# RMSNorm and matmul on one core: the first eight output tiles in one store in place of two

## Chip, core and metric

The kernel runs on one core of a Trainium2 chip. The metric is device time in microseconds (us). Before the change the median of three runs is 209.02 us (208.88 to 209.29).

## What is computed

Each of 16 x 1024 = 16,384 tokens has 512 features. A token is divided by the root of its mean square, scaled by gamma, and multiplied by a 512 x 768 weight matrix, all inputs and outputs in f32:

```python
def reference(x, gamma, weight, eps):
    rms = np.sqrt(np.mean(x ** 2, axis=-1, keepdims=True) + eps)
    x_norm = x / rms * gamma
    return np.matmul(x_norm, weight).astype(np.float32)
```

33.6 MB of tokens come in and 50.3 MB of results go out, so besides the arithmetic a good 85 MB pass through the core's 16 DMA engines.

## The kernel before

**Tiles.** The tokens are cut into NT = 128 tiles of 128 tokens, one token per partition. Tiles 2j and 2j+1 are pair j, and the main loop runs over pairs. A tile is loaded as f32 (`xt`), cast to bf16 by GpSimd (`xb`, line 189), transposed by TensorE as f32 words that each hold two bf16 (line 231), copied from PSUM to `xT` by VectorE (`evac`, line 240), multiplied with the weights in eight matmuls (line 300) into one of three PSUM accumulators taken in turn, and scaled by 1/rms on the way out of PSUM into `ot` (`scale`; even tiles on ScalarE, line 279, odd tiles on VectorE, line 281). ScalarE also makes the sums of squares (line 197) and the square roots (line 202). Gamma is multiplied into the weights at the start.

**Quads.** From tile 28 on, the last four of every 16 tiles (28 to 31, 44 to 47, ..., 124 to 127) take another way to their transposed form: GpSimd casts all four into `xq` (`cast_quad`, line 260), and VectorE transposes them in 16 blocks (`move_quad`, line 271), three blocks at the head of each pair, before the pair's other VectorE work. The quad of tiles 124 to 127 is cast at pair 55 and first moved at pair 56, which is tiles 112 and 113.

**Loads.** `x_first` and `x_size` say which tiles travel together: tiles 0 to 3, tiles 4 to 7, and from then on eight tiles a transfer. The loads of the first 32 tiles and the weights are issued on SP (SyncE) at the start; later ones on ScalarE's queue, in ScalarE's program order, when the pair loop reaches them (`load_until`). `xt` holds two blocks of 16 tiles.

**Stores.** `o_first` and `o_size` do the same for the output. When the last tile of a group is scaled, `store` issues the group's transfer on SP, from one of four `ot` buffers of eight tiles. SP issues in order and a wait of one store holds only later stores. `finish_tile` makes the last tile of a group also wait for the tile before it.

**Which token is where.** `rows` gives the view of `x` or of `out` for a transfer: within a block of `t` tiles, partition p holds `t` tokens that lie side by side in memory. The same function serves loads and stores, so a tile has the same tokens in both. A partition's share of a load is 2 KB a tile, of a store 3 KB a tile.

**The order of instructions** is written out by hand: each operation is recorded with the cells that it reads and writes (class `Order`), and semaphore waits are derived from them; no scheduler moves anything.

Of the kernel before, what the change touches and what calls it, by code (L numbers as in the profile page):

```python
# [100 lines left out]
def kernel(  # L101
# [22 lines left out]
    XG, OG = 16, 8  # L124
# [3 lines left out]
    def stretches(group, parts):  # L128
        first, size, i = {}, {}, 0
        for g in range(NT // group):  # L130
            for n in parts.get(g, [group]):
                for t in range(i, i + n):
                    first[t], size[t] = i, n
                i += n
        return first, size

    last = NT // OG - 1
    x_first, x_size = stretches(OG, {0: [4, 4]})
    o_first, o_size = stretches(OG, {0: [4, 4], last - 1: [4, 4], last: [4, 2, 2]})

    def rows(ap, i, n):
        base, t = (i - i % OG, OG) if OG <= i < XG else (x_first[i], x_size[i]) if i < OG else (i - i % XG, XG) if i < 2 * XG else (i - i % (2 * XG), 2 * XG)
        return ap[base * P:(base + t) * P, :].rearrange("(p t) d -> p t d", t=t)[:, i - base:i - base + n, :]

    def sb(name, shape, dtype):
# [29 lines left out]
    def load(i):  # L175
        dst, to = x_of(i, x_size[i])
        queue = SP if i < FIRST else ACT
        order.transfer(queue, lambda: queue.dma_start(out=dst, in_=rows(x, i, x_size[i])), writes=to)
# [109 lines left out]
    def store(i):  # L288
        first, n = o_first[i], o_size[i]
        s = first // OG % OTS  # L290
        if i == first + n - 1:
            src = ot[s][:, first % OG:first % OG + n, :]
            order.transfer(SP, lambda: SP.dma_start(out=rows(out, first, n), in_=src), reads=cells("ot", s, first % OG, n))
# [188 lines left out]
```

## Time and profile before

| | |
|---|---|
| median of the runs | 209.02 us |
| the profiled execution, its own time | 208.72 us |
| its span, first to last instruction | 206.8 us |
| TensorE busy | 193.7 us (94%) |
| VectorE busy | 149.3 us (72%) |
| ScalarE busy | 144.8 us (70%) |
| GpSimd busy | 60.2 us (29%) |
| DMA | 85.62 MB, 414 GB/s over the span |
| granted TensorE clock | 0.987 |
| stores | 13 of 3072 KB, 5 of 1536 KB, 2 of 768 KB, all on SP |
| loads on ScalarE's queue | 12 of 2048 KB, median 19.4 us from issue to landing |

Engines are PE (TensorE matmul), PEld (its weight load), DVE (VectorE), ACT (ScalarE), POOL (GpSimd) and SP (SyncE). Line numbers such as L281 are those of the kernel before. The profile numbers the DMA queues: q1 is SP's, q10 is ScalarE's. A transfer is spread over the 16 DMA engines, eight partitions to each; a partition's share moves as one piece, which the trace records with start, duration and size. Times are counted from the start of the span. The median time from issue to landing contains the time that a transfer stands in its queue.

### The profile page before, as it was taken

The page shows a single profiled execution, that of the slowest core. Times are in us where ns is not written, and L with a number is a line of the kernel's source. Part 1 is how long each engine was busy: PE and PEld are TensorE (multiplying, and loading weights), DVE is VectorE, ACT ScalarE, POOL GpSimd, SP SyncE. Part 2 cuts the span into 40 slices and gives each one's busy share as a digit, 9 for nine tenths or more (in the row PEclk, how much of TensorE's full clock was granted, in tenths as well). Part 3 has the DMA queues.
Part 4 walks back from the last instruction along what each step waited for, and adds up shares of the span by engine and source line. Part 5 has one row for each costly group of instructions (what it writes and reads, how often), then busy time and mean ns, then how long its engine had stood idle before and what let it go on. Part 6 is the DMA issues. An engine that isn't in the chain of part 4 may idle for free.

```text
span 206.8 us, 2750 instructions
## 1 busy us (share of the span) xinstructions
PE 193.7 (94%) x1212; PEld 72.8 (35%) x717; DVE 149.3 (72%) x255; ACT 144.8 (70%) x343; POOL 60.2 (29%) x34
## 2 busy tenths in 40 slices
PE   7799999999999999999999999999999999999920
PEld 0244433433433333433343333343343334343300
DVE  0446557998579966999579975999569974999410
ACT  2698998877777687777787687677877688663310
POOL 1437733154206250153305160060704206000000
PEclk9999999999999999999999999999999999999995
DMA  5999999999999999999999999999999999999992
GB/s 206 426 436 437 393 390 431 428 445 429 436 425 415 441 434 431 439 428 425 418 431 442 417 444 415 441 428 425 444 428 420 441 428 431 433 428 416 423 412 103
DMA packets 5632, 85.62 MB, mean 414 GB/s; under 512 B 626, under 2 KB 628, under 8 KB 1140
## 3 DMA queue, kind: packets, MB, share of 16 engines
q1 hardware_dynamic: 3888, 60.29, 68.8%
q10 hardware_dynamic: 1732, 25.17, 28.5%
q8 instruction: 7, 0.11, 0.2%
q14 instruction: 5, 0.04, 0.0%
HBM read 35.13 MB, written 50.33 MB: 413 GB/s over the span
## 4 chain that ended last, share of the span: by engine, by line
PE 91%; DMA 2%; DVE 1%; issue 1%; ACT 1%; SPq 0%
PE ps L300 80%; PE ps L231 10%; DMA xt<-in_x_dram 2%; DVE ot L281 0%; ACT jk L197 0%; DVE xT L240 0%; DVE w_bf L281 0%; ACT ssq L202 0%; DVE rstd L204 0%; SPq L477 0%; SPq L436 0%
## 5 line engine op out<-in xcount | busy, mean ns | idle before, releaser
L300 PE MATMUL ps<-w_bf,xT 128*128 128x256 bf16 (+1 forms) x783 | 145.1, 326 | 1.1 <-DVE w_bf L281 0.2
L279 ACT ACTIVATE ot<-ps,rstd 128x768 f32<-128x768 f32 x64 | 57.7, 901 | 46.2 <-PE ps L300 46.1
L197 ACT ACTIVATE jk<-xt 128x512 bf16<-128x512 f32 x128 | 78.9, 620 | 3.1 <-DMA xt<-in_x_dram 3.1
L189 POOL CAST xb<-xt 128x2048 bf16<-128x2048 f32 (+3 forms) x21 | 46.4, 2221 | 108.3 <-DMA xt<-in_x_dram 56.5
L281 DVE TENSOR_SCALAR ot<-ps,rstd 128x768 f32<-128x768 f32 x64 | 64.8, 1013 | 9.7 <-PE ps L300 9.2
L296 PEld LDWEIGHTS <-xT 128*128 128x128 bf16 x400 | 39.3, 98 | 59.4 <-issue 57.9
L231 PE MATMUL ps<-ident_f,xb 128*128 128x128 f32 x200 | 54.4, 276 | 1.1 <-POOL xb L189 1.1
L240 DVE COPY xT<-ps 128x1024 bf16<-128x1024 bf16 (+1 forms) x53 | 34.5, 653 | 25.5 <-PE ps L231 24.9
L271 DVE STREAM_TRANSPOSE xTq<-xq 32x256 f32<-32x256 f32 x112 | 48.7, 435 | 1.9
L231 PEld LDWEIGHTS ps<-ident_f,xb 128*128 128x128 f32 x200 | 28.2, 143 | 46.5 <-issue 43.6
L300 PE MATMUL ps<-w_bf,xTq 128*128 128x256 bf16 (+1 forms) x217 | 41.8, 324 | 0.4
L197 ACT ACTIVATION_READ_ACCUMULATOR jk<-xt 128x1 f32 x128 | 24.5, 192 | 0.0
L296 PEld LDWEIGHTS <-xTq 128*128 128x128 bf16 x112 | 11.0, 98 | 14.5 <-issue 14.5
L260 POOL CAST xq<-xt 128x2048 bf16<-128x2048 f32 x7 | 13.3, 1896 | 4.6 <-DVE xTq L271 4.6
L204 DVE RECIPROCAL rstd<-ssq 128x8 f32<-128x8 f32 (+3 forms) x20 | 3.9, 193 | 7.5 <-ACT ssq L202 7.4
L202 ACT ACTIVATE ssq<-ssq,eps_sb 128x8 f32<-128x8 f32 (+3 forms) x20 | 6.0, 302 | 0.6
L300 PE MATMUL ps<-ot 128*128 128x512 bf16 x10 | 4.8, 628 | 1.4 <-DVE eps_sb L354 1.4
L279 ACT ACTIVATE w_bf<-ot,g_sb 128x768 bf16<-128x768 f32 x2 | 1.9, 937 | 1.1 <-DMA ot<-in_weight_dram 1.1
L377 DVE COPY g_sb<-ps 128x4 f32<-128x4 f32 x1 | 0.2, 161 | 3.1 <-PE ps L371 3.1
L341 ACT ACT_TABLE_LOAD x1 | 1.3, 1283 | 1.5 <-SPq L436 1.5
L281 DVE TENSOR_SCALAR w_bf<-ot,g_sb 128x512 bf16<-128x512 f32 (+2 forms) x3 | 1.4, 483 | 0.6 <-DMA ot<-in_weight_dram 0.6
L371 PEld LDWEIGHTS ps<-ident_f,ot 2*128 2x128 f32 x2 | 0.3, 200 | 2.6 <-issue 2.6
(10 smaller groups left out, 2.0 us busy)
## 6 DMA issues: line engine op xcount, KB each, us to landing
out_dram<-ot SPq DMA_DIRECT2D x13, 3072.0 KB, 23.9
xt<-in_x_dram ACTq DMA_DIRECT2D x12, 2048.0 KB, 19.4
out_dram<-ot SPq DMA_DIRECT2D x5, 1536.0 KB, 10.8
xt<-in_x_dram SPq DMA_DIRECT2D x3, 2048.0 KB, 18.4
xt<-in_x_dram SPq DMA_DIRECT2D x2, 1024.0 KB, 7.3
ot<-in_weight_dram SPq DMA_DIRECT2D x2, 768.0 KB, 7.0
out_dram<-ot SPq DMA_DIRECT2D x2, 768.0 KB, 7.3
ot<-in_gamma_dram ACTq DMA_DIRECT2D x1, 2.0 KB
```

The costliest lines, as they stand in the source:

```text
L189: run(POOL, lambda: POOL.tensor_copy(out=xb[s][:, i % 8:i % 8 + n, :], in_=src), of, cells("xb", s, i % 8, n))
L197: run(ACT, lambda: ACT.activation(out=jk[n], in_=src[:, 0, :], func=AF.Square, accum_out=ssq[:, i:i + 1]), of, [("jk", n), ("ssq", i)])
L202: run(ACT, lambda: ACT.activation(out=ssq[:, s], in_=ssq[:, s], func=AF.Sqrt, scale=1.0 / D, bias=eps_sb), [("ssq", t) for t in range(i, i ...
L204: run(DVE, lambda: DVE.reciprocal(out=rstd[:, s], in_=ssq[:, s]), [("rms", i)], [("rstd", t) for t in range(i, i + n)])
L231: run(PE, lambda: PE.transpose(out=tp[b][:, t, h, :], in_=words[:, lo:lo + P], identity=ident_f), cells("xb", s, j % 4 * 2 + t) + ["ident" ...
L240: run(DVE, lambda: DVE.tensor_copy(out=dst[:, t:t + n, :], in_=src[:, t:t + n, :]), [("tp", b)], cells("xT", j % XTS, t, n))
L260: run(POOL, lambda: POOL.tensor_copy(out=xq, in_=src), of, ["xq"])
L271: run(DVE, lambda: DVE.transpose(out=dst, in_=src), ["xq"], [("xTq", n)])
L279: run(ACT, lambda: ACT.mul(out=dst, in_=src, mul=r), reads, writes)
L281: run(DVE, lambda: DVE.tensor_single_scalar(out=dst, in_=src, scalar=r, op=mybir.AluOpType.mult), reads, writes)
L296: run(PE, lambda: PE.ldweights(lhsT), of)
L300: run(PE, lambda: PE.add_instruction(mybir.InstMatmult(name=nc.get_next_instruction_name(), engine=mybir.EngineType.PE, ins=[PE.lower_ap(r ...
```

## The change

Tiles 0 to 7 are stored by one transfer of 3072 KB, issued when tile 7 is ready, where tiles 0 to 3 and 4 to 7 were stored by two of 1536 KB. For this the eight tokens of a partition must lie side by side in memory, so the view in `rows` changes for tiles 0 to 7: a block is now eight tiles. It holds for the loads too. Tiles 0 to 7 are still loaded by two transfers of four tiles (`x_first`, `x_size` are as they were), but each now takes one half of every partition's eight tokens: pieces of 8 KB that lie 16 KB apart, where they adjoined. The instructions of TensorE, VectorE, ScalarE and GpSimd are the same ones in the same order; SP has one store less. Tile 3 is no longer the last of a group, so its scaling no longer waits for tile 2.

```diff
     last = NT // OG - 1
     x_first, x_size = stretches(OG, {0: [4, 4]})
-    o_first, o_size = stretches(OG, {0: [4, 4], last - 1: [4, 4], last: [4, 2, 2]})
+    o_first, o_size = stretches(OG, {last - 1: [4, 4], last: [4, 2, 2]})
 
     def rows(ap, i, n):
-        base, t = (i - i % OG, OG) if OG <= i < XG else (x_first[i], x_size[i]) if i < OG else (i - i % XG, XG) if i < 2 * XG else (i - i % (2 * XG), 2 * XG)
+        base, t = (i - i % OG, OG) if i < XG else (i - i % XG, XG) if i < 2 * XG else (i - i % (2 * XG), 2 * XG)
         return ap[base * P:(base + t) * P, :].rearrange("(p t) d -> p t d", t=t)[:, i - base:i - base + n, :]
```

## The prediction, made before the changed kernel was run

> **What bounds the kernel now.** I read the page's busy slices and its chain of waits first, then busy time by stretch, then the stores at the end. In the slices (40 of them, tenths busy) TensorE's row and the DMA row are both full; the chain of waits names TensorE.
>
> ```profile
> PE   7799999999999999999999999999999999999920
> DMA  5999999999999999999999999999999999999992
> PE 91%; DMA 2%; DVE 1%; issue 1%; ACT 1%; SPq 0%
> ```
>
> The chain follows instructions and can't see that a transfer stands in line behind others. The stretches can (columns: stretch and its length, busy time and instructions of PE, PEld, DVE, ACT and POOL, granted clock, DMA share, GB/s):
>
> ```profile
> 22.70:24.20 1.50, 1.45 (x12) 0.59 (x7) 1.50 (x3) 0.99 (x4) 1.50 (x1) 1.00 1.00 426
> 24.20:27.30 3.10, 3.10 (x23) 1.28 (x14) 1.65 (x3) 3.10 (x9) 1.41 (x1) 1.00 0.98 308
> 110.00:170.00 60.00, 59.63 (x383) 22.52 (x224) 50.12 (x85) 45.67 (x111) 18.28 (x7) 1.00 1.01 431
> 170.00:198.00 28.00, 27.50 (x175) 9.95 (x100) 20.49 (x35) 15.62 (x32) 3.73 (x2) 1.00 1.00 425
> 198.00:205.50 7.50, 0.00 (x0) 0.00 (x0) 0.77 (x1) 0.00 (x0) 0.00 (x0) 0.72 0.64 265
> ```
>
> The DMA share is 0.98 to 1.01 up to 198 us, at 425 to 431 GB/s apart from one dip, and TensorE has nothing left after 198. What fills 198 to 205.5 is a line of stores. The last two, by issue time and by time to landing:
>
> ```profile
> 196.20 0.33 SPq L293 DMA_DIRECT2D out_dram<-ot  x1
> out_dram<-ot SPq DMA_DIRECT2D x1, 768.0 KB, 7.8
> 199.06 0.33 SPq L293 DMA_DIRECT2D out_dram<-ot  x1
> out_dram<-ot SPq DMA_DIRECT2D x1, 768.0 KB, 6.8
> ```
>
> They land at 204.0 and 205.9, 1.9 us apart, though issued 2.9 apart. The records of single transfers say why: a DMA engine moves one partition's 6 KB of these stores in 0.234 us, eight make 1.88 us. Read engine by engine, all 16 move data without a pause from 3 us to about 202; most end between 202 and 203.6 and one, which also fetches instructions, ends at 205.41. That engine sets the end. Its eight pieces of the last store start at 203.53; issued at 199.06, and with the 1.0 us from issue to first data that the first load shows (0.95 to 1.95), they could have started at 200.06. So **TensorE has about 3.4 us of slack** to the end: 3.5 by the last store, 3.4 by the store issued at 193.59 (starts 197.96). The time is set by the bytes, and by anything that leaves that DMA engine idle.
>
> **The change part by part.** *Removed:* one store issue on SP (0.33 us, SP otherwise waits: nothing), one completion write per DMA engine (0.009 us each), and VectorE's wait on ScalarE at tile 3 (ScalarE had long finished tile 2: nothing). *Merged:* per DMA engine 16 pieces of 12 KB at 0.4613 us (7.38) become 8 pieces of 24 KB at 0.9154 (7.32), by the mean of such pieces in this trace: 0.06 us less. With the completion write, **-0.07 us**.
>
> *Loads of tiles 0 to 7:* still two transfers in pieces of 8 KB, but now 16 KB apart instead of adjoining. No row shows that. The nearest: pieces of 16 KB that adjoin (tiles 8 to 15) and that lie 32 KB apart (tiles 16 to 31) both take 0.613 us. I take nothing; the bound is one more slow start like that of the first loads (2 to 4 us; 0.5 us over the normal 0.309 a piece, summed over 16 engines), so 0 to +0.5.
>
> *Later issue:* tiles 0 to 3 were stored at 16.99; now they wait for tile 7 and go at 24.18. Behind that instruction on SP stand only later stores; all loads from tile 32 on are on ScalarE's queue. What hides the 7.2 us is the queue itself: the load of tiles 24 to 31 is ahead on SP.
>
> ```profile
> xt<-in_x_dram SPq DMA_DIRECT2D x1, 2048.0 KB, 25.1
> 16.99 0.35 SPq L293 DMA_DIRECT2D out_dram<-ot  x1
> 24.18 0.34 SPq L293 DMA_DIRECT2D out_dram<-ot  x1
> ```
>
> It was issued at 4.03 and landed at 29.1, and the first 12 KB piece of any store moves at 26.48. The merged store's pieces are ready at 24.18 + 1.0 = 25.2, so 1.3 us before their turn: no idle, nothing. Without that cover the engines would stand idle from the end of the loads to 25.2.
>
> The Trainium skill (Perfetto Trace Analysis, DMA Optimizations) says that splitting a DMA may let parts start sooner, where the DMA engines are generally idle. That speaks against merging; here the DMA share is 1.00 at 22.7 to 24.2, so the condition fails and by the row the split store gained no start.
>
> *Turns, the part that matters:* where SP's and ScalarE's queues both hold work, an engine takes a piece of each in turn. With 12 KB store pieces (30 to 36 us) and with 24 KB ones (46 to 54 us):
>
> ```profile
> q10 hardware_dynamic: 98, 1.51, 58.6%
> q1 hardware_dynamic: 102, 1.07, 41.8%
> ...
> q1 hardware_dynamic: 82, 2.02, 58.8%
> q10 hardware_dynamic: 88, 1.44, 42.4%
> ```
>
> q10 is the loads: 1.4 times the stores' bytes, then 0.7 times, which is 16/12 and 16/24. The loads of tiles 32 to 39 and 40 to 47 had 16 pieces per engine paired with 12 KB pieces; now with 24 KB ones. Both landed later by up to 16 x 0.454 = 7.3 us; two store pieces went ahead of the first load piece (27.60), which leaves 14 x 0.454 = 6.4; if the load now starts before the later store, among the last four pieces of tiles 24 to 31, it is 2 to 3. I take **6 us** (range 2 to 7.3). Both queues stay full to the last load, so every later load is late by the same 6, and the stores are some 5 earlier. Early loads have 10 us of slack; it shrinks from load to load, since a load comes every 12.2 us and TensorE uses one in 11.7. The last one (tiles 120 to 127, issued 146.57, landing 170.23) is the one that hurts:
>
> ```profile
> 170.35 1.90 POOL L189 CAST xb<-xt 128x2048 bf16<-128x2048 f32 x1 [8.78 <-DMA xt<-in_x_dram]
> 172.19 1.90 POOL L260 CAST xq<-xt 128x2048 bf16<-128x2048 f32 x1
> 176.41 1.32 DVE L271 STREAM_TRANSPOSE xTq<-xq 32x256 f32<-32x256 f32 x3
> 177.91 0.69 DVE L240 COPY xT<-ps 128x1024 bf16<-128x1024 bf16 x1 [0.18 <-PE ps L231]
> 178.52 1.01 DVE L281 TENSOR_SCALAR ot<-ps,rstd 128x768 f32<-128x768 f32 x1
> ```
>
> The second cast ends at 174.09, 2.32 us before VectorE wants it. Six us later, VectorE stands 3.7 us; then come three transposes, a copy and tile 113's scaling (3.02 us), ending at 179.43 + 3.7 = 183.1. TensorE needs that accumulator for tile 116 at about 181.5 (181.51 + the last row of tile 115). So TensorE waits 1.6 us (2.9 at 7.3 us, none under 4.4), and never makes it up. Against the 3.4 us of slack this costs **nothing**: the stores come 1.6 us later into a line that is still full.
>
> The sum: -0.07 + 0 + 0 + 0. The profiled execution took 208.72 (span 206.77, 1.95 around it), so 208.65; that run lies 0.30 under the median of 209.02, so on the median's scale 208.95, said as **209.0**.
>
> **The rivals.** *Late loads reach the end (slower).* Place: VectorE's wait for the quad cast of tiles 124 to 127. VectorE is nearly full there (3.02 of some 3.1 us a pair of tiles), so the 2.0 us between tile 113's scaling and tile 116 may be gone by earlier stalls (tiles 104 to 111 come within 3.7 us of the same wait). Then TensorE loses the whole 3.7 to 5.0 us, and over 3.4 it shows: +0.3 to +1.6, 209.3 to 210.6. It decides from a TensorE delay of 3.4 us. For it: no engine can make time up. Against: my 2.0 us. Chance 0.28.
>
> *The dip goes (faster).* From 24.2 to 27.3 the DMA moved 308 GB/s instead of 426: load pieces took up to 1.29 us instead of 0.61, in all 0.82 us per engine. It starts as ScalarE's first load and SP's second store arrive, with the first store waiting. If that meeting causes it and it goes: -0.82, 208.2. Against: ScalarE's load is unchanged, a store still arrives at 25.2, and later meetings show no dip. It might also double, +0.8. Chance 0.15 for gone.
>
> *TensorE's chain sets the end, as the page has it (slower).* Then 1.6 to 2.9 us show in full: 210.6 to 211.9. Against: the 6.8 us landing behind other stores. 0.05.
>
> *Splitting did start the store sooner (slower).* The queue runs dry before 25.2, and up to one 4-tile store, 8 x 0.461 = 3.7 us, is lost: 212.7. Against: 1.3 us of cover. 0.02. The rule beside it is that of the Trainium skill named above (Perfetto Trace Analysis, DMA Optimizations).
>
> **How the numbers follow.** No change 0.50, the rivals as given. A measurement of this kernel can tell 0.2% (0.42 us). Faster 0.15; same 0.50; slower 0.28 + 0.05 + 0.02 = 0.35. The likeliest case's own range is 208.6 to 209.4 (bound of the loads' price and the runs' spread). The range is 208.2 (dip gone) to 210.6 (late loads, upper end); outside lie the two last rivals and the doubled dip beside late loads.
>
> **What would show it.** Right: one 3072 KB store at 24.2 with its first data near 27; loads from tile 40 on landing about 6 us later; VectorE waiting for the quad cast near 176; TensorE ending 1 to 3 us later; the last store's time to landing shorter by as much; the end unmoved. Wrong: DMA share under 1 near 25; the last store landing about 3.3 us after issue (backlog spent); or 24.2 to 27.3 at 426 GB/s.

## The result, and the profile after

The changed kernel takes 210.29 us in the median of ten runs (208.95 to 214.15), beside 209.04 for ten of the kernel before (208.74 to 209.29). The ratio is 1.0061 with a 95% interval of 1.0042 to 1.0079: **slower by some 0.6%, or 1.3 us**, where the forecast was no change. The time lies in the range given, on the side of the first rival. Its ten runs spread over 5.2 us, the ten of the kernel before over 0.55 (in later, larger sets that kernel has two runs of 210.70). Ratios leave out runs more than 1.5% above the fastest of their kernel, so where runs scatter the median can say more than the ratio.

The profiled execution took 210.82 (span 208.7), 2.1 more than before. The page's slices of TensorE, the granted clock, DMA and its rate:

```profile
PE   7499999999999999999999999999999999999930
PEclk9759999999999999999999999999999999999995
DMA  6999999999999999999999999999999999999992
GB/s 212 426 443 427 405 264 432 418 432 427 429 426 430 446 426 432 415 446 421 424 441 429 430 430 427 429 426 432 426 427 432 421 435 426 433 443 405 407 413 121
```

Two things are new: a clock of 0.7 and 0.5 in the second and third slice, and one slice (26 to 31 us) at 264 GB/s. The same slice stood at 390 before. By stretch, in the columns of the prediction's table:

```profile
24.20:27.30 3.10, 3.05 (x22) 1.28 (x14) 1.70 (x3) 2.57 (x8) 1.82 (x2) 1.00 0.85 291
27.30:31.50 4.20, 4.20 (x30) 1.70 (x18) 2.40 (x4) 4.20 (x13) 3.69 (x2) 1.00 0.94 289
110.00:170.00 60.00, 59.58 (x383) 22.65 (x225) 50.83 (x86) 44.92 (x109) 18.26 (x7) 1.00 1.00 428
170.00:198.00 28.00, 27.79 (x178) 10.28 (x103) 21.25 (x36) 16.82 (x36) 3.73 (x2) 1.00 0.99 425
198.00:207.40 9.40, 2.14 (x14) 0.50 (x6) 1.61 (x2) 0.90 (x1) 0.00 (x0) 0.76 0.74 309
```

Of the kernel before, the second of these stretches:

```profile
27.30:31.50 4.20, 4.15 (x29) 1.64 (x17) 2.00 (x4) 4.08 (x13) 2.29 (x2) 1.00 1.02 436
```

From 24.2 to 31.5 us the kernel before moved 3.10 x 308 + 4.20 x 436 = 2786 KB, the changed one 3.10 x 291 + 4.20 x 289 = 2116. At 428 GB/s the missing 670 KB are **1.6 us** of all DMA engines, most of the 1.9 us by which the last data come later (207.33 instead of 205.41). From 110 to 198 us the rates are the same within 1%.

Why that stretch is thin is seen in two issue times:

```profile
25.69 0.36 ACTq L178 DMA_DIRECT2D xt<-in_x_dram  x1
26.61 0.35 SPq L293 DMA_DIRECT2D out_dram<-ot  x1
```

The first load on ScalarE's queue went at 23.28 before, the store of tiles 4 to 7 at 24.18, and a store of tiles 0 to 3 had long been in line. Here TensorE ran at half clock early and tile 7 was 2.4 us late; the loads on SP had all been moved by 26.1 (a few stragglers up to 26.7 aside), and nothing was in line but that load of ScalarE's, whose data moved from 26.68 on. The engines stood idle for part of the time (0.94 us each on the mean from 20 to 36 us), and the load's pieces of 16 KB took 0.92 us on the mean where 0.61 is usual. The first store data moved at 31.45.

The end is as before: the last store still stands in a line, and TensorE has slack.

```profile
201.49 0.33 SPq L293 DMA_DIRECT2D out_dram<-ot  x1
out_dram<-ot SPq DMA_DIRECT2D x1, 768.0 KB, 6.3
```

6.3 us to landing (6.8 before), of which eight pieces of 0.234 us are 1.9.

The turns came out near what was reckoned (1.7 times the loads' bytes here, where 24/16 is 1.5). Queue shares from 32.5 to 38.5 us, where the store's pieces are now 24 KB:

```profile
q1 hardware_dynamic: 66, 1.62, 62.9%
q10 hardware_dynamic: 74, 0.95, 37.1%
```

The last load's data end 4.3 us later than before (173.1 instead of 168.8). But TensorE is 2.4 us late itself, so VectorE does not wait for the quad cast in this execution:

```profile
174.49 1.89 POOL L189 CAST xb<-xt 128x2048 bf16<-128x2048 f32 x1 [8.87 <-DMA xt<-in_x_dram]
176.32 1.89 POOL L260 CAST xq<-xt 128x2048 bf16<-128x2048 f32 x1
178.84 1.32 DVE L271 STREAM_TRANSPOSE xTq<-xq 32x256 f32<-32x256 f32 x3
```

The second cast ends at 178.2, the move starts at 178.8, without a bracket for idle time.

### The profile page after: what moved, and what is told of

Same layout as the page of the kernel before. It is cut to its first block, busy times and chain, and to the rows that moved or that the text cites. A ratio compares the mean times of both kernels' runs of the same rounds, so it can differ in the third digit from the quotient of the medians.

```text
span 208.7 us, 2746 instructions
## 1 busy us (share of the span) xinstructions
PE 194.8 (93%) x1212; PEld 73.2 (35%) x717; DVE 149.4 (72%) x255; ACT 144.6 (69%) x343; POOL 60.0 (29%) x34
## 4 chain that ended last, share of the span: by engine, by line
PE 91%; DMA 3%; DVE 1%; issue 1%; ACT 1%; SPq 0%
PE ps L300 80%; PE ps L231 10%; DMA xt<-in_x_dram 3%; DVE ot L281 0%; ACT jk L197 0%; DVE xT L240 0%; DVE w_bf L281 0%; ACT ssq L202 0%; DVE rstd L204 0%; SPq L477 0%; SPq L436 0%
## 5 line engine op out<-in xcount | busy, mean ns | idle before, releaser
L300 PE MATMUL ps<-w_bf,xT 128*128 128x256 bf16 (+1 forms) x783 | 147.1, 329 | 1.7 <-DVE w_bf L281 0.8
L300 PE MATMUL ps<-ot 128*128 128x512 bf16 x10 | 4.2, 557 | 1.4 <-DVE eps_sb L354 1.4
```

The lines of the kernel that those rows point to most:

```text
L300: run(PE, lambda: PE.add_instruction(mybir.InstMatmult(name=nc.get_next_instruction_name(), engine=mybir.EngineType.PE, ins=[PE.lower_ap(r ...
```

## The experiments

Three theories were on the table. **A**: the late issue does it, because no store stands in SP's queue when the loads end. **B**: the order of tokens does it (B1: of the loads). **C**: the turns do it, by late loads that stall VectorE at the quads. Times are medians of 7 to 12 runs, long ones included; each ratio is against the kernel before on the same chip.

| kernel | us | ratio (95%) |
|---|---|---|
| changed | 210.29 | 1.0061 (1.0042 to 1.0079) |
| e1: one late store, old order, 12 KB pieces | 209.25 | 1.0023 (1.0012 to 1.0034) |
| e2: new order, two stores in time | 209.43 | 1.0021 (1.0008 to 1.0035) |
| e3: changed, ScalarE's first load earlier | 209.16 | 1.0023 (1.0008 to 1.0039) |
| e4: changed, two more warm-up matmuls | 210.32 | 1.0048 (1.0028 to 1.0068) |
| e5: before, loads 16 KB apart | 209.42 | 1.0019 (1.0008 to 1.0031) |
| e6: changed, loads as before | 209.78 | 1.0040 (1.0015 to 1.0066) |
| e7: before, both stores late | 209.22 | 1.0026 (1.0005 to 1.0047) |
| e8: e1, store 3 us later still | 209.12 | 1.0011 (1.0000 to 1.0021) |
| e9: changed, two late stores of 12 KB pieces | 210.03 | 1.0054 (1.0029 to 1.0080) |
| b3: before, ScalarE's first load earlier | 210.33 | 1.0034 (1.0000 to 1.0068) |

What each profile showed, one execution each, on several chips, against the one profile of the kernel before: landing of the load of tiles 0 to 3; how late tile 8 and tile 115 were scaled against the kernel before; when the last load's data ended, against before; the time that a DMA engine lost in three stretches, on the mean of 16 (idle, or a piece over its usual time: 0.234, 0.309, 0.460, 0.612 and 0.913 us for 6, 8, 12, 16 and 24 KB; from 0 to 6 us only the pieces are counted); and the last data.

| profile (its time) | load 0-3 lands | tile 8 / 115 late | last load late | lost 0-6 / 20-36 / 36-198 | last data |
|---|---|---|---|---|---|
| before (208.72) | 5.86 | 0 / 0 | 0 | 0.52 / 0.87 / 0.64 | 205.41 |
| changed (210.82) | 6.22 | 2.4 / 2.4 | 4.3 | 0.61 / 2.62 / 1.05 | 207.33 |
| changed, a1 (209.62) | 6.02 | 1.2 / 1.2 | 3.6 | 0.67 / 1.36 / 0.81 | 206.20 |
| changed, a2 (210.00) | 6.14 | 0.9 / 2.7 | 5.4 | 0.64 / 1.47 / 1.59 | 206.71 |
| changed, a3 (210.19) | 6.06 | 1.1 / 1.6 | 4.1 | 0.66 / 1.53 / 0.68 | 206.70 |
| changed, a4 (210.64) | 6.13 | 1.3 / 3.0 | 5.6 | 0.71 / 1.39 / 1.81 | 207.30 |
| e1 (208.98) | 5.76 | 0.5 / 0.5 | -0.7 | 0.45 / 1.28 / 0.61 | 205.67 |
| e2 (209.63) | 6.24 | 0.5 / 0.5 | 0.8 | 0.7 / 1.2 / 0.6 | 206.19 |
| e3 (209.14) | 6.01 | 0.5 / 0.5 | 2.1 | 0.61 / 1.06 / 0.63 | 205.68 |
| e4 (209.41) | 6.15 | 1.3 / 1.3 | 2.4 | 0.5 / 1.4 / 0.8 | 205.93 |
| e5 (209.87) | 6.20 | 0.4 / 0.4 | 0.1 | 0.73 / 1.22 / 0.52 | 206.41 |
| e6 (210.15) | 5.70 | -0.2 / 3.6 | 6.2 | 0.18 / 1.38 / 2.46 | 206.86 |
| e7 (211.35) | 5.75 | 0.9 / 0.9 | 2.2 | 0.4 / 1.1 / 1.5 | 208.12 |
| e8 (209.12) | 5.77 | 0.1 / 0.1 | -0.6 | 0.41 / 1.40 / 0.60 | 205.72 |
| e9 (210.09) | 6.19 | 1.6 / 1.6 | 3.3 | 0.7 / 1.3 / 1.3 | 206.82 |
| b3 (209.03) | 5.81 | 0.2 / 0.2 | 0.2 | 0.5 / 0.8 / 1.1 | 205.64 |
| b4 (209.99) | 6.34 | 1.5 / 1.5 | 2.4 | 0.6 / 0.7 / 1.7 | 206.80 |
| b5 (214.93) | 5.73 | 1.9 / 5.5 | 8.2 | 0.79 / 0.46 / 5.01 | 211.66 |

In the five profiles of the changed kernel the three losses together exceed those of the kernel before by 2.25, 0.81, 1.67, 0.84 and 1.88 us; the last data came 1.92, 0.79, 1.30, 1.29 and 1.89 later. So in these five the bookkeeping of the DMA engines accounts for the result. It does less well elsewhere: the sums miss the shift by 0.5 to 0.6 us in e5 and e6, and by 1.7 and 2.0 in e7 and b5, the two long executions, where the engine that ended last was 4.1 and 4.3 us behind the mean of the 16 (before: 2.45). A mean over the engines can't show that.

**Late issue or order of tokens? e1 and e2.** e1 keeps the old order and gives the one store two pieces of 12 KB per partition:

```diff
+            if first == 0:
+                src = src.rearrange("p (b t) d -> p b t d", b=2)
+                dst = out[:OG * P, :].rearrange("(b p t) d -> p b t d", b=2, p=P)
```

> One store of tiles 0 to 7, as in the changed kernel, but with the old order of tokens: the loads of tiles 0 to 7 are pieces of 8 KB that adjoin, and the one store moves two pieces of 12 KB per partition. Theory A (the late issue does it: when the loads of the first 32 tiles have passed, no store stands in SP's queue, and the DMA engines run short of work between about 24 and 31 us): slower than before by about as much as the changed kernel, 209.6 to 210.3 us, with a stretch under 350 GB/s after 25 us. Theory B (the order of tokens does it: loads in pieces 16 KB apart land later, and the clock drops early): 209.0 us, like the kernel before.

e2 is the changed kernel with the old line of `o_first`:

```diff
-    o_first, o_size = stretches(OG, {last - 1: [4, 4], last: [4, 2, 2]})
+    o_first, o_size = stretches(OG, {0: [4, 4], last - 1: [4, 4], last: [4, 2, 2]})
```

> The new order of tokens with two stores: tiles 0 to 3 are stored as soon as they are ready, in pieces of 12 KB that lie 24 KB apart. Theory A: 209.0 us within 0.3, since a store stands in SP's queue when the loads end, even where the clock drops early and tile 7 is late. Theory B: 210.0 to 210.5 us, as the changed kernel. The profile shows with either whether the load of tiles 0 to 3 lands near 6.2 us (the changed kernel) or 5.9 us (before).

Each costs 0.2%, about a third of the whole. Neither theory had it alone. e1 shows little scatter (11 of 12 runs from 208.95 to 209.41), e2 much (208.68 to 211.88).

**Is it what was queued? e3.** `START` goes from 4 to 3, so that ScalarE issues the load of tiles 32 to 39 at 20.2.

> The changed kernel, with the first load on ScalarE's queue (tiles 32 to 39) issued one pair earlier, about 3 us sooner. Theory A: that load is in its queue before the loads on SP end, so the DMA engines have work while the merged store is awaited; most of the loss goes: 209.0 to 209.5 us and no idle near 25 us. Theory B: 210.3 us, unchanged. My forecast's rival (late loads hold TensorE at the end) also expects a gain here, as every load lands earlier, but would show TensorE waiting near 176 us in the changed kernel.

209.16: two thirds of the loss are gone. The stretches of e3:

```profile
24.20:27.30 3.10, 3.10 (x22) 1.24 (x13) 2.09 (x4) 2.74 (x8) 1.56 (x1) 1.00 1.01 418
27.30:31.50 4.20, 4.15 (x28) 1.70 (x17) 1.68 (x3) 4.14 (x12) 0.00 (x0) 1.00 1.03 351
```

Together 2770 KB, within 20 of the kernel before. The same edit also made the loads only 2.1 to 2.7 us late, so it helps A and C alike and does not tell them apart.

**Is it the clock? e4.** `warm_up(2)` ahead of the first transposes becomes `warm_up(4)`.

> The changed kernel with four warm-up matmuls in place of two ahead of the first transposes, so that TensorE stands idle for about 0.7 us instead of 1.7 us before them. If the early clock drop (0.5 from about 8 to 14 us in the profiled run) makes the loss by making tile 7 late: granted clock 1.00 in 5 to 16 us, the merged store issued near 24.4 instead of 26.6 us, time 209.0 to 209.4 us with little scatter. If the loss does not hang on the clock: 210.3 us with the clock at 1.00.

A miss. The clock stood at 0.57 from 9 to 13 us all the same, and the median stayed; two of the seven runs took 215.59 and 218.67. What the early clock costs was not isolated in this way. The mean clock of a whole run doesn't settle it either: of the runs of the kernel before, one with a mean clock of 0.973 took 208.81 and one with 0.969 took 210.70, and where in the run the clock was low is not recorded.

**The loads alone, the store alone: e5 and e6.** In e5 only the loads of tiles 0 to 7 have the new view, in e6 only the store:

```diff
+        if ap is x and i < OG:
+            base, t = 0, OG                  (e5)
+            base, t = x_first[i], x_size[i]  (e6)
```

> The kernel before with one part of the change alone: the loads of tiles 0 to 7 take pieces of 8 KB that lie 16 KB apart; both stores are as before (so tokens of tiles 0 to 7 come out in another order than the reference's). Theory B1 (the loads' new order brings the scatter and the later start): the load of tiles 0 to 3 lands near 6.1 to 6.2 us, most runs 208.7 to 209.3, some at 210 and above, median 209.2 to 209.5. Theory A (only the late issue of the store costs time): 208.9 us and no run above 209.4.

> The changed kernel with the loads of tiles 0 to 7 as before (pieces that adjoin), so that only the merged store with its pieces of 24 KB is left of the change (tokens of tiles 0 to 7 come out in another order than the reference's). Theory A: like the merged store with the old order of tokens, 209.1 to 209.4 us, little scatter. Theory B1: 208.9 us, as before. If the size of the pieces made the difference instead: 210 us, like the changed kernel.

e5: B1 holds in the median and in the landing; only one of the twelve runs is above 210. The load of tiles 0 to 3 lands at 6.20. With the new order it landed from 6.01 to 6.24 in all ten profiles taken; with the old order from 5.70 to 5.86 in seven of eight (6.34 in one). e6 costs 0.40%, more than e1 with its smaller pieces, though the intervals overlap. Its profile is the clearest picture of theory C. GpSimd's casts and VectorE's work (one line number is two higher here):

```profile
176.42 1.89 POOL L191 CAST xb<-xt 128x2048 bf16<-128x2048 f32 x1 [8.97 <-PE ps L302]
178.26 1.89 POOL L262 CAST xq<-xt 128x2048 bf16<-128x2048 f32 x1
```

```profile
176.69 1.01 DVE L283 TENSOR_SCALAR ot<-ps,rstd 128x768 f32<-128x768 f32 x1
180.19 1.33 DVE L273 STREAM_TRANSPOSE xTq<-xq 32x256 f32<-32x256 f32 x3 [2.48 <-POOL xq L262]
...
182.14 1.01 DVE L283 TENSOR_SCALAR ot<-ps,rstd 128x768 f32<-128x768 f32 x1
```

The bracket is the wait: VectorE stands 2.48 us for the quad cast, which stood behind the load (issued at 146.39, landed 29.9 us later, at 176.3). In all it waits 5.1 us for quad casts, at three places, where it waited for none before, and tile 115 is 3.6 us late.

**Merging or lateness? e7, and the dose, e8.** e7 keeps two stores, both issued after tile 7:

```diff
+        if i == 3:
+            return
+        for first, n in ([(0, 4), (4, 4)] if i == 7 else [(first, n)]):
...
-                           reads=cells("ot", s, first % OG, n))
+                           reads=cells("ot", s, first % OG, n) + cells("ot", s, i % OG))
```

> The kernel before with both stores kept, but the store of tiles 0 to 3 issued only when tile 7 is ready, just ahead of that of tiles 4 to 7. Theory A (the late issue, not the merging): 209.1 to 209.4 us, as with the merged store. Against it (merging as such, one transfer of 3 MB): 208.9 us, as before.

e8 is e1 with the store held until tile 9:

```diff
+        if i == 7:
+            return
+        if i == 9:
...
+            order.transfer(SP, lambda: SP.dma_start(out=dst, in_=src), reads=cells("ot", 0, 0, 8) + cells("ot", 1, 1))
```

> The merged store with the old order of tokens, issued 3 us later, after tile 9 (near 27.5 us, when the loads on SP have ended). This is the dose test of theory A: the stretch in which the DMA engines move loads alone grows by some 3 us, at 300 to 350 GB/s instead of 428, with up to 1 us idle: 0.8 to 2 us slower than the merged store issued after tile 7, so 210.0 to 211.3 us. If the lateness costs nothing: 209.25 us.

Two late stores cost what one late store costs (1.0026 and 1.0023), so merging as such is not the cause of that part. But the dose test **failed**: issued at 26.95 instead of 24.70, the store cost no more. The stretches of e8:

```profile
24.20:27.30 3.10, 3.10 (x23) 1.28 (x14) 1.71 (x4) 3.10 (x9) 1.31 (x1) 1.00 1.00 349
27.30:31.50 4.20, 4.20 (x30) 1.69 (x18) 1.94 (x4) 4.08 (x13) 3.57 (x2) 1.00 0.97 353
```

2565 KB, 0.5 us less than before, and 0.2 us idle: here the clock held, and ScalarE's load went at 23.32 and its data moved from 25.8 on. Lateness of the store costs a few tenths. Where the load is late as well, as in the changed kernel's first profile (25.69), the engines stood idle for 0.94 us; in the other four it was issued at 24.2 to 24.5, and they stood idle for 0.2 us or less.

**The size of the pieces: e9.** The changed kernel with e7's edit: new order, late, 12 KB pieces.

> The changed kernel, order of tokens and late issue included, but with the merged store cut again into two transfers, both issued when tile 7 is ready, so that a store's pieces are 12 KB. Theory C (turns: 24 KB pieces beside the first two loads on ScalarE's queue make every later load about 5 us late, and in runs where TensorE is not late itself, VectorE then waits for the quad casts at the end): loads from tile 40 on at most 1 us later than in the kernel before, no wait of VectorE for a quad cast, 209.2 to 209.6 us. If the size of the pieces has no part in it: as the changed kernel, 210 us and more.

Half a hit. From tile 48 on the loads were 1.2 to 1.7 us later, about what tile 8 was late (1.6), and only the last was 3.3 later, and VectorE waited for no quad cast, as C has it. But the time, 210.03, is near the changed kernel's. So the turns of 24 KB pieces are not needed for a loss of this size (0.54%, 0.29 to 0.80); the order of tokens and the late issue together can make most of it.

**More executions of the changed kernel: a1 to a4.**

> The changed kernel once more, for a second profile of it. Theory C: if the granted clock stays 1.00 from 7 to 16 us, the tiles run within 0.5 us of the kernel before up to tile 96, then VectorE waits for the quad casts and TensorE ends 1 to 3 us later; if the clock drops early, the tiles are 1 to 2.5 us late from tile 8 on and nothing waits for a quad cast. In both the last data are written after 205.6 us. Theory A alone: the time comes from 24 to 32 us, and no VectorE wait shows.

> The changed kernel a third time, for one more profile: as for the second.

> The changed kernel, one more profile, to see where its longer executions lose the time. If the scatter comes from the stretch of loads alone between 20 and 36 us: in a run of 211 us or more the data pieces of that stretch cost over 2.5 us a DMA engine (the kernel before 0.9). If it comes from single DMA engines that fall behind later: that stretch stays under 1.7 us, and the slowest engine ends more than 3 us after the mean of the 16.

> The changed kernel again, with the same two readings as the look before: over 2.5 us lost between 20 and 36 us, or the slowest DMA engine more than 3 us after the mean.

Tile 8 was 0.9 to 1.3 us late in all four, and against the expectation for a1 and a2 a late start and a wait for the quad can go together. In a2, a3 and a4 VectorE waited 2.2, 0.6 and 1.8 us for quad casts; in a1 and the first profile not at all. In a2:

```profile
177.43 1.90 POOL L260 CAST xq<-xt 128x2048 bf16<-128x2048 f32 x1
...
179.36 1.33 DVE L271 STREAM_TRANSPOSE xTq<-xq 32x256 f32<-32x256 f32 x3 [1.93 <-POOL xq L260]
```

None of the four fell on an execution of 211 us or more, so these profiles don't tell the two readings of the long executions apart. The profile of e7 (211.35) fits one of them: it lost 1.1 us from 20 to 36, and its slowest DMA engine ended 4.1 us after the mean, which is the second reading.

**A better kernel? And the long executions: b3, b4, b5.** The kernel before with `START` 3.

> The kernel before with the first load on ScalarE's queue issued one pair earlier, about 3 us sooner. It would beat the kernel before if the stretch from 24 to 27 us, in which loads go at 308 GB/s, came from that load meeting the second store: 208.2 us. If the bytes set the time and nothing is idle: 208.9 us, no change.

> The kernel before with the first load on ScalarE's queue one pair earlier (208.9 to 216 us in its runs), one more profile. Same two readings: a long stretch of loads alone between 20 and 36 us, or DMA engines that fall behind later.

> The kernel before with the earlier load again, with the same two readings as the look before: over 2.5 us lost between 20 and 36 us, or the slowest DMA engine more than 3 us after the mean.

b3 met neither expectation: half of its runs lie between 210.9 and 216.1, with the edit that helped the changed kernel in e3. Its dip was smaller (400 GB/s from 24.2 to 31.5 us, where the kernel before has 382), and its best run is 208.85, so a smaller dip alone made nothing faster. b4 took 209.99. b5 caught a long execution, 214.93, and the second of the two readings fits again: it lost least of all from 20 to 36 us (0.46) and 5.0 us between 36 and 198, and its slowest DMA engine ended 4.3 us after the mean of the 16 (211.66, mean 207.32; before: 205.41 and 202.96, 2.45 apart). GpSimd's last casts, VectorE's wait for the second of them, a stretch near the end, and the last store:

```profile
178.36 1.89 POOL L189 CAST xb<-xt 128x2048 bf16<-128x2048 f32 x1 [9.24 <-DMA xt<-in_x_dram]
180.19 1.89 POOL L260 CAST xq<-xt 128x2048 bf16<-128x2048 f32 x1
```

```profile
182.12 1.33 DVE L271 STREAM_TRANSPOSE xTq<-xq 32x256 f32<-32x256 f32 x3 [3.04 <-POOL xq L260]
```

```profile
190.00:198.00 8.00, 7.54 (x47) 2.36 (x24) 7.78 (x13) 2.68 (x3) 0.00 (x0) 1.00 0.76 321
```

```profile
204.04 0.33 SPq L293 DMA_DIRECT2D out_dram<-ot  x1
out_dram<-ot SPq DMA_DIRECT2D x1, 768.0 KB, 8.0
```

The last load is 8.2 us late, VectorE stands 3.04 us for the quad cast, tile 115 is 5.5 us late, beyond the 3.4 us of slack, and then the DMA share falls to 0.76 from 190 to 198: on most engines the stores come too late and the engine runs dry. This is the first rival's chain, in another kernel than the changed one, but it does not set the end. The last store took 8.0 us to landing (6.8 before). The other 15 engines ended by 209.5, 14 of them by 207.0, and on the one that ended at 211.66 the eight pieces of the last store start only at 209.82, 5.8 us after the issue: by the prediction's own reckoning 4.8 us of slack were left there. What set this end is an engine that had fallen behind. Single slow pieces are at hand as a reason: of the 24 KB store pieces 84 took more than 1.1 us, instead of 0.91. Before it was 5, in the changed kernel's first profile 14, in a1 and a3 4, in a2 32, in a4 28, in e6 49, in e7 26, in b4 30. The time doesn't follow their number alone (b4 with 30 took 209.99, a4 with 28 took 210.64), and what makes them slow is open.

## Why the prediction was wrong

*What bounds the kernel.* Right. Bytes and idle DMA engines set the end: the sums of lost time match the shift of the last data within half a microsecond in the five profiles of the changed kernel. TensorE was up to 3.0 us late in the changed kernel and the last store still took 6 us to land.

*Merged pieces, -0.07.* The price of a piece was right: 24 KB pieces at 0.917 us in the changed kernel, 0.915 before. A gain of 0.07 us is too small for these runs to show.

*Loads of tiles 0 to 7, "I take nothing".* This step **failed**. Pieces 16 KB apart cost 0.19% by themselves (e5): the first load lands 0.34 us later in e5, and in nine of the ten profiles with this order the first six microseconds lose 0.1 to 0.2 us more than before. The rows that I leaned on, 16 KB pieces at 0.613 us, were of later loads and larger pieces; which of the two makes the difference was not tested. The bound of +0.5 did hold the loss (its 0.5 us is the mean of the 16 engines, not their sum, as the prediction has it).

*Later issue, "no idle, nothing".* This step **failed** too; in the profiles of the changed kernel it is the larger one, in the ratios (e1 0.23%, e5 0.19%) the two are alike. The cover was 1.3 us, worked out from one execution in which the clock held; in the changed kernel tile 8 was 0.9 to 2.4 us late in five of five profiles, the store went at 25.1 to 26.6 instead of 24.2, and its first data moved at 29.6 to 31.5 and not near 27. From 20 to 36 us the engines lost 0.5 to 1.8 us more than before. The term that was mis-sized is the 1.0 us from issue to first data, taken from the first load, when the engines were free: for the late store it was 4.1 to 4.8 us in these five profiles. It fails without a late clock as well: in e6 the store went at 24.00, even sooner than reckoned, and its first data moved at 28.36, 4.4 us later, not at 26.48 (the loads ahead of it on SP ended at 27.6); from 20 to 36 us 0.5 us more was lost. Late issue alone costs 0.1 to 0.3% (e1, e7, e8).

The rule of the Trainium skill that the prediction set aside (Perfetto Trace Analysis, DMA Optimizations) says two things: "Splitting DMAs into smaller chunks may allow some to start sooner", and that with generally idle DMA engines the overall task may complete sooner. The prediction read the idle engines as the condition for both. The runs differ from that condition: the engines were busy at 1.00 (22.7 to 24.2 us), and storing the first half early was still worth some 0.2% (e1, e7). By the profiles this is because the early part was in the queue when the other work ran out.

*Turns.* Right in kind, and nearly in size in e6, where TensorE was on time at first: every load from tile 40 on was 4.8 to 6.2 us late where 6 was said. In the changed kernel it was 2.9 to 5.6, part of that TensorE's own lateness (e9, with 12 KB pieces: 1.2 to 1.7 from tile 48 on to the last load but one). The load of tiles 32 to 39 was only 0.4 to 0.7 us late. Its data moved before the late store's (25.7 to 26.7 against 29.6 to 31.5), which is the case that the prediction named for 2 to 3 us and did not take. VectorE's wait at the quad was there in three of five profiles. *"Nothing", since 3.4 us of slack cover it*, held for TensorE's end: the last store was issued 1.1 to 2.5 us later than before in the changed kernel and 3.0 in e6, and on the engine that ended last its pieces still stood in line, with 1.9 us of slack left where it was least (e6). But e6, a2 and a4 lost 1.0 to 1.8 us more than before after 36 us, about half of it in pieces slower than usual and the rest idle after 170 us, so whether the turns were free is not shown.

*The rivals.* None of them is the whole. The dip did not go; it grew, which stood at the end of that rival as a doubling of +0.8. The queue running dry, given 0.02, is part of what happened in the first profile, where 0.94 us were idle from 20 to 36 us. Late loads reached VectorE, but in no profile did they set the end, b5 included.

*What stays open.* Three parts of about 0.2% each (loads apart, late issue, and what 24 KB pieces add: e6 over e1) come to the measured 0.6%, but their intervals are about half as wide as they are, and the third is not clear of noise. The early clock drop was seen in all five profiles of the changed kernel, and in e1, e3, e4, e7 and b5, not in the other eight; whether it belongs to the change was not settled. A variant with new order, whole store and a clock that holds was not obtained. In e9, with two late stores, the recorded clock held, and tile 8 was late and the time 210.09 all the same.

## What to carry to other kernels

Where the DMA engines are the bound, ask of a store not when its data are needed but what else would be in the queue at that moment: an early small store that only waits in line is the cover for the moment when the loads run out. Work such a margin out against a bad execution (a late clock, a late first load), not against the one on the page; 1.3 us was less than the kernel's own scatter (tile 8 was 1.5 us late in b4, which has nothing of the change). When the sizes of pieces on one queue change, work out the turns of the other queue to the last transfer, and test the cover there.

## What the runs showed of the hardware

A queue that gets work while the other is moving data can wait long for its first turn: ScalarE's load of 23.28 moved at 27.60 before, at 23.87 for an issue at 20.21 in e3, and SP's store of 26.61 at 31.45 in the changed kernel. With the other queue all but empty it was 1.0 us (25.69 to 26.68). The wait is no constant: in ten other profiles with a late store, ScalarE's first load, issued at 23.10 to 24.86, moved at 25.5 to 25.9, 1.0 to 2.5 us after its issue (e8: 23.32 to 25.79). The late stores waited 3.6 to 5.2 us in all twelve profiles that have one.

Load pieces slow down in that interval. In the changed kernel's first profile the 16 KB pieces from 26.6 to 31.4 took 0.92 us on the mean and up to 1.62, and 0.61 again as soon as store pieces moved between them; before, 0.92 from 24.2 to 26.5. Loads alone are not the reason, since up to 24 us they took 0.615. What is the reason was not found.

The granted clock can fall to half early and the time not show it. From 9 to 13 us, the changed kernel and the one before:

```profile
9.00:11.00 2.00, 1.79 (x6) 0.43 (x3) 1.03 (x3) 1.10 (x3) 0.00 (x0) 0.50 1.01 427
11.00:13.00 2.00, 2.00 (x9) 0.45 (x4) 0.17 (x1) 1.46 (x5) 0.49 (x1) 0.50 1.08 463
```

```profile
9.00:11.00 2.00, 2.00 (x10) 0.53 (x5) 0.68 (x2) 1.38 (x3) 0.00 (x0) 1.00 1.03 434
11.00:13.00 2.00, 1.96 (x14) 0.90 (x9) 0.80 (x3) 1.97 (x7) 0.85 (x1) 1.00 1.05 446
```

TensorE got through 13 matmuls (transposes among them) instead of 22 in those 4 us, at a clock of 0.50, and the DMA moved as much as before. (The column PE adds up to 15 and 24, since what is under way at 11 us stands in both rows.) e1 had the same drop (0.50 from 9 to 11 us) and took 208.98.

A granted clock of 1.00 in the profile does not mean that TensorE ran at full speed. The first matmuls with the real weights in e9 (its line numbers differ) and in the kernel before:

```profile
9.17 3.78 PE L305 MATMUL ps<-w_bf,xT 128*128 128x512 bf16 x11 [0.17 <-DVE w_bf L281]
```

```profile
8.85 3.04 PE L300 MATMUL ps<-w_bf,xT 128*128 128x512 bf16 x14 [0.17 <-DVE w_bf L281]
```

The recorded clock is 1.00 from 6 to 20 us in both. But in e9 TensorE's weight loads come 0.64 us apart from 9.55 to 12.11, and 0.33 us apart in the kernel before from 10.31 to 11.29. Tile 8 is 1.6 us late in e9; b4, where weight loads come 0.64 us apart as well under a recorded 1.00, has it 1.5 us late.
